# Hybrid encoder trunk on one core: gate tiles kept in DRAM until paced steps take them, and queries, keys and probabilities turned by DRAM and 32x32 block transposes in place of tensor-engine transposes

## The chip, the core and the metric

The kernel runs on one core of a Trainium2 chip. The core has a tensor engine (PE, with its weight loads shown as PEld), a vector engine (DVE), a scalar engine (ACT), GpSimd (POOL), a sync engine (SP, which issues the weight loads) and 16 DMA engines. Each engine takes its instructions in one fixed order. The metric is the device time of one execution in microseconds, the median of several runs. Before the change it is 1943.53 us (three runs, 1942.93 to 1944.33).

## What is computed

Two layers, each over 256 tokens of width 2048 in float32. One input projection feeds a convolution branch and an attention branch; both are gated, projected, merged and projected again.

```python
def conv_branch(a, glu, gate, conv_w, conv_b, ln_g, ln_b):
    u = a * jax.nn.sigmoid(glu)
    u = lax.conv_general_dilated(u, conv_w[:, None, :], ...) + conv_b   # depthwise, causal, width 31
    u = jax.nn.silu(layernorm(u, ln_g, ln_b))
    return u * jax.nn.silu(gate)

def mla_branch(...):
    q = (rmsnorm(q_down, q_a_g) @ w_uq).reshape(B, S, 16, 192)
    kv = (rmsnorm(kv_down, kv_a_g) @ w_ukv).reshape(B, S, 16, 128 + 128)
    ...                       # shared rotary key, per-head norm of q and k, rotary on the last 64
    o = chunk_causal_attention(q, k, v)
    return o.reshape(B, S, 2048) * jax.nn.silu(gate)

def hybrid_layer(x, ...):
    proj = rmsnorm(x, norm_g) @ w_in
    ...
    y = jax.nn.sigmoid(g_conv) * y_conv + jax.nn.sigmoid(g_mla) * y_mla
    return x + y @ w_out
```

## The kernel before

Tokens are two tiles of 128 (`t`), the model's width 16 tiles of 128. Every large product is taken in float32r from split operands: a value is a high part `hi` (a float32r cast) and a low part `lo` (value minus `hi`), and a product is three matmuls, hi by hi, hi by lo and lo by hi (lines 217 to 219). `product` (line 205) does one block of up to 512 columns. It goes through K in steps of two tiles; a step is called a slot here: 12 matmuls, then `background()`. Before each slot `split` makes the weights' halves from the loaded tile `raw`: ACT casts `hi` (line 178), DVE subtracts `lo` (line 179). `hi` and `lo` have three buffers each, and splits are issued two slots ahead, with a raised priority. In a layer the splits are numbered in order, 344 to a layer: 24 for the down block, then 8 for GLU block 0, and for each pair of heads `b` 2 for `uq`, 2 for `ukv` and 8 for the next GLU block; then 8 for each of the 28 blocks of the gates and output products. In the text, lo118 is the low half for split 118.

A framework records the instructions, orders them on each engine by priority and by times of its own, and fixes that order when the kernel is built. It also places the semaphores. `tc.issue_after(ins)` keeps instructions behind `ins` on its engine.

Work beside the products comes in two queues. `background()` (line 191) runs one step of `attn` at every slot, and as much of `fill` as a budget allows: `budget["rate"]` is added per slot, and every step has a cost. `fill` holds the convolution's taps (`tap`, line 634; two DVE operations of 128x256 each, line 646) and the layer norm (`mean`, `centre`, `var`, `apply`). What is left of `fill` is drained before the first `cgate` block.

There are two ways to turn a tile from tokens-on-partitions to channels-on-partitions. `turn` (line 230) writes the tile to DRAM by four DMAs on GpSimd (line 237), fetches it by a fifth (line 242), and at a later split, put in `deferred`, a DVE transpose of 32x32 blocks (line 246) ends it. GLU products and most gate blocks use it. The other way is PE: a matmul with the identity into PSUM, then a split copy out of PSUM.

Attention of a pair is eight steps at eight slots: `stats` (norm factors, scaled keys, rotary parts), `turn_rope` and `turn_nope` for queries and for keys (PE transposes at lines 526 and 513, then the splits), `scores`, `turn_p` (PE transposes of the probabilities, lines 588 to 592, then splits) and `values`. The last block of each set of gates (`turn4`, `c == 3`) also goes by PE (line 714).

The evacuations `uq_evac` and `ukv_evac` copy queries, keys and values of a pair out of the accumulators, of which there are four; the tiles `q`, `k` and `r` have two buffers.

Of the kernel before, what the change touches and what calls it, by code (L numbers as in the profile page):

```python
# [59 lines left out]
TURNED_AFTER = 6  # L60
SUMS_AFTER = 1
# [34 lines left out]
def trunk(ctx: ExitStack, tc: tile.TileContext, xT, x, g_in, pos, win, wuq, wukv, wpc, wpm, wo, cst, rows, invf, out):  # L96
# [13 lines left out]
    turn_d = pool("turn", 4, space=bass.MemoryType.DRAM)  # L110
    acc_p = pool("acc", 4, space=PSUM)
# [27 lines left out]
    for l in range(DEPTH):  # L139
# [12 lines left out]
    loaded, done = {}, {}  # L152
# [16 lines left out]
    def split(i):  # L169
# [10 lines left out]
        done[i] = hi, lo  # L180
        while deferred and deferred[0][0] <= i:
            with tc.issue_after(ins.ins):
                deferred.popleft()[1]()
# [5 lines left out]
    budget = {"fill": 0.0, "rate": 0.0}  # L189
# [40 lines left out]
    def turn(src, n, use, dst=None):  # L230

        e = n // 4
        d = turn_d.tile([4, 32, 4, e], F32, tag=f"t{n}", name="turn_d")
        for i in range(4):
# [3 lines left out]
            )  # L240
        z = wide_p.tile([P, 4, n // P, 32], F32, tag="w", name="turned")
        nc.gpsimd.dma_start(z.rearrange("p i c s -> p (i c s)"), d.rearrange("j s i e -> (j s) (i e)"))
# [119 lines left out]
    for l in range(DEPTH):  # L362
# [85 lines left out]
        def pair_of(b, pairs=pairs, v_split=v_split):  # L448
            if b not in pairs:
                pairs[b] = dict(  # L450
                    q=work2.tile([P, T, 2, QK], F32, tag="q", name="q"),
                    k=work2.tile([P, T, 2, NOPE], F32, tag="k", name="k"),
                    r=work2.tile([P, 2, T, 2, ROPE], F32, tag="r", name="r"),
# [6 lines left out]
        def uq_evac(b, t, ps, pair_of=pair_of):  # L460
            p = pair_of(b)
            nc.scalar.copy(p["q"][:, t].rearrange("p h d -> p (h d)"), ps)
            for h in range(2):
                junk = work.tile([P, 512], F32, tag="junk", name="junk")
                nc.scalar.activation(
                    junk[:, :QK], ps[:, h * QK : (h + 1) * QK], AF.Square, accum_out=p["ss"][:, 0, t, h : h + 1]
                )

        def ukv_evac(b, t, ps, pair_of=pair_of):
            p = pair_of(b)  # L470
            v = ps.rearrange("p (h a d) -> p h a d", h=2, a=2)
            nc.scalar.copy(p["vh"][:, t], v[:, :, 1, :])
            nc.vector.tensor_sub(p["vl"][:, t], v[:, :, 1, :], p["vh"][:, t].bitcast(F32))
            nc.scalar.copy(p["k"][:, t], v[:, :, 0, :])
            for h in range(2):
                junk = work.tile([P, 512], F32, tag="junk", name="junk")
                nc.scalar.activation(junk[:, :NOPE], v[:, h, 0, :], AF.Square, accum_out=p["ss"][:, 1, t, h : h + 1])

        def attention(b, pair_of=pair_of, ss_d=ss_d, kpe=kpe, ccq=ccq, ssq_t=ssq_t, gqk=gqk, nope_t=nope_t, rope_t=rope_t, rope_k=rope_k, rope_l=rope_l, o_sb=o_sb, pt_h=pt_h, pt_l=pt_l, rinv=rinv):
# [3 lines left out]
            def stats():  # L483
                ss, q, k = p["ss"], p["q"], p["k"]
# [7 lines left out]
                rk = r[:, 1].unsqueeze(3)  # L492
                nc.vector.tensor_mul(k, k, rk.broadcast_to([P, T, 2, NOPE]))
                nc.vector.tensor_mul(
                    p["r"][:, 1], kpe.unsqueeze(2).broadcast_to([P, T, 2, ROPE]), rk.broadcast_to([P, T, 2, ROPE])
                )
                qr = q[:, :, :, NOPE:]
                qa = work.tile([P, T, 2, ROPE], F32, tag="qa", name="qa")
                qb = work.tile([P, T, 2, ROPE], F32, tag="qb", name="qb")
                nc.vector.tensor_mul(qa, qr, ccq.unsqueeze(2).broadcast_to([P, T, 2, ROPE]))  # L500
                nc.vector.tensor_mul(qb, qr, ssq_t.unsqueeze(2).broadcast_to([P, T, 2, ROPE]))
                qr = p["r"][:, 0]
                nc.vector.tensor_sub(qr[:, :, :, :HALF], qa[:, :, :, :HALF], qb[:, :, :, HALF:])
                nc.vector.tensor_add(qr[:, :, :, HALF:], qb[:, :, :, :HALF], qa[:, :, :, HALF:])
# [3 lines left out]
            def turn_nope(which):  # L508
                src = p["qk"[which]]
                tp = tp_p.tile([P, 2, SEQ], F32, tag="tp", name="tp_qk")  # L510
                for h in range(2):
                    for t in range(T):
                        nc.tensor.transpose(tp[:, h, t * P : (t + 1) * P], src[:, t, h, :NOPE], ident)  # L513
                hi, lo = nope_t[:, 2 * which], nope_t[:, 2 * which + 1]
                if which == 0:
                    nc.scalar.activation(hi, tp, AF.Copy, scale=gqk)
                    nc.vector.scalar_tensor_tensor(lo, tp, gqk, hi.bitcast(F32), op0=ALU.mult, op1=ALU.subtract)
                else:
                    nc.scalar.copy(hi, tp)
                    nc.vector.tensor_sub(lo, tp, hi.bitcast(F32))  # L520

            def turn_rope(which):
                src = p["r"][:, which]
# [298 lines left out]
        for kind, i, pl in planned:  # L822
# [28 lines left out]
            elif kind == "mgate":  # L851
                budget["rate"] = 0.85
                if i == 3:
                    drain(attn)
# [103 lines left out]
```

## Time and profile before

| | |
|---|---|
| median of three runs | 1943.53 us (1942.93 to 1944.33) |
| the profiled execution | 1944.69 us, of which the span is 1942.9 |
| PE busy | 1927.0 us, 99% |
| DVE busy | 1583.7 us, 82% |
| ACT busy | 1096.6 us, 56% |
| GpSimd busy | 222.7 us, 11% |
| mean granted PE clock | 0.996 |

How to read the lines. A line of a timeline is start and duration in us, engine, source line, operation, the tile written and those read, shapes and count; in brackets stands the engine's idle time just before it and what ended it. A line of a group is the operation with its count, then busy time in us and mean ns of one, then idle time before it. A line of waits is who waited for whom: us in total, times, longest. A line of windows is the stretch, its length, then busy us and count for PE, PEld, DVE, ACT and POOL, then the granted clock, the share of the DMA engines and GB/s. Matmuls are pipelined, so their durations overlap, and their starts tell more.

### The profile page before, as it was taken

Reading aid. Unit: us, or ns where it says so; the run is one execution under the profiler, and the core shown is the slowest. Engines: PE = TensorE matmul, PEld = TensorE weight load, DVE = VectorE, ACT = ScalarE, POOL = GpSimd, SP = SyncE. Lnnn points to the kernel's source line nnn. Section 1 sums busy time; section 2 is a strip of 40 time slices with the busy share of each in tenths; the row PEclk is TensorE's granted clock in tenths of the full one; section 3 lists DMA queues with packets and bytes.
Section 4 is the critical chain, followed back from the end, with each engine's and each line's share of the span. In section 5 each row is a group of like instructions: output and inputs, shape, how many; then the busy total and the mean of one; then the engine's idle time right before and its main releaser. Section 6 shows DMA issues by size and latency. Waiting matters only on the chain.

```text
span 1942.9 us, 25501 instructions
## 1 busy us (share of the span) xinstructions
PE 1927.0 (99%) x9085; PEld 1627.9 (84%) x9085; DVE 1583.7 (82%) x2816; ACT 1096.6 (56%) x1745; POOL 222.7 (11%) x424
## 2 busy tenths in 40 slices
PE   9999999999999999999999999999999999999999
PEld 8888888888888887888898888888888888878887
DVE  7789988999998787666657899889999987876654
ACT  6667767665444446444556676776554434454443
POOL 0111111121000001121301121121200000022200
PEclk9999999999999999999999999999999999999999
DMA  8655545566555555666865455555665555566674
GB/s 292 217 178 182 195 167 180 197 217 222 195 195 195 195 195 186 231 243 229 277 230 197 176 195 177 179 182 195 225 210 195 194 195 195 181 210 231 241 255 141
DMA packets 71760, 397.72 MB, mean 205 GB/s; under 512 B 12736, under 2 KB 12752, under 8 KB 32720
## 3 DMA queue, kind: packets, MB, share of 16 engines
q1 hardware_dynamic: 55728, 361.44, 52.7%
q0 software_dynamic: 15904, 34.65, 5.6%
q8 instruction: 71, 1.16, 0.2%
q14 instruction: 57, 0.47, 0.1%
HBM read 375.59 MB, written 20.45 MB: 204 GB/s over the span
## 4 chain that ended last, share of the span: by engine, by line
PE 97%; DVE 1%; DMA 1%; issue 0%; ACT 0%; SPq 0%; POOL 0%; DVEq 0%
PE acc L218 31%; PE acc L219 31%; PE acc L217 31%; PE o_ps L604 1%; PE s L558 1%; PE tp_qk L513 1%; DMA turned<-turn_d 0%; DVE lo L179 0%; DVE v_t L672 0%; PE tp_rope L526 0%; DMA raw<-in_win 0%; PE s L544 0%; PE tp L714 0%; PE s L542 0%; PE tp_p L588 0%
## 5 line engine op out<-in xcount | busy, mean ns | idle before, releaser
L178 ACT CAST hi<-raw 128x1024 fp32r<-128x1024 f32 (+2 forms) x688 | 704.6, 1025 | 726.8 <-PE acc L219 507.2
L179 DVE TENSOR_TENSOR lo<-raw,hi 128x1024 fp32r<-128x1024 f32 (+2 forms) x688 | 815.6, 1188 | 268.7 <-ACT hi L178 265.9
L646 DVE SCALAR_TENSOR_TENSOR v_t<-u_t,cst,v_t 128x256 f32<-128x256 f32 x960 | 413.9, 478 | 1.1
L218 PE MATMUL acc<-lo,h_hi 128*128 128x512 f32 (+2 forms) x864 | 334.8, 388 | 1.4 <-DVE lo L179 1.4
L218 PE MATMUL acc<-lo,hT 128*128 128x512 f32 (+2 forms) x864 | 333.7, 386 | 2.4 <-DVE lo L179 2.4
L219 PE MATMUL acc<-hi,h_lo 128*128 128x512 f32 (+2 forms) x864 | 332.4, 385 | 0.0
L219 PE MATMUL acc<-hi,hT 128*128 128x512 f32 (+2 forms) x864 | 331.6, 384 | 0.0
L217 PE MATMUL acc<-hi,h_hi 128*128 128x512 f32 (+2 forms) x864 | 303.7, 386 | 4.8 <-ACT hi L178 4.8
L217 PE MATMUL acc<-hi,hT 128*128 128x512 f32 (+2 forms) x864 | 303.1, 384 | 1.6 <-ACT hi L178 1.6
L217 PEld LDWEIGHTS acc<-hi,h_hi 128*128 128x128 f32 x864 | 162.3, 189 | 35.1 <-ACT hi L178 5.6
L218 PEld LDWEIGHTS acc<-lo,hT 128*128 128x128 f32 x864 | 162.7, 188 | 32.5 <-DVE lo L179 3.6
L218 PEld LDWEIGHTS acc<-lo,h_hi 128*128 128x128 f32 x864 | 163.3, 189 | 31.8 <-DVE lo L179 2.7
L217 PEld LDWEIGHTS acc<-hi,hT 128*128 128x128 f32 x864 | 161.6, 188 | 31.6 <-ACT hi L178 2.1
L219 PEld LDWEIGHTS acc<-hi,h_lo 128*128 128x128 f32 x864 | 163.5, 189 | 29.2
L219 PEld LDWEIGHTS acc<-hi,hT 128*128 128x128 f32 x864 | 162.8, 188 | 29.1
L237 POOL DMA_DIRECT2D turn_d<-gate x160 | 87.0, 550 | 571.4 <-ACT gate L769 345.0
L237 POOL DMA_DIRECT2D turn_d<-su x128 | 69.6, 550 | 477.9 <-DVE su L626 467.7
L218 PE MATMUL acc<-lo,yT 128*128 128x512 f32 x256 | 100.0, 390 | 0.0
L218 PE MATMUL acc<-lo,ycT 128*128 128x512 f32 x256 | 99.6, 390 | 0.0
L219 PE MATMUL acc<-hi,yT 128*128 128x512 f32 x256 | 99.6, 389 | 0.0
L218 PE MATMUL acc<-lo,oT 128*128 128x512 f32 x256 | 99.6, 389 | 0.0
L219 PE MATMUL acc<-hi,oT 128*128 128x512 f32 x256 | 99.6, 389 | 0.0
(204 smaller groups left out, 2487.6 us busy)
## 6 DMA issues: line engine op xcount, KB each, us to landing
raw<-in_win SPq DMA_DIRECT2D x192, 1024.0 KB, 4.8
raw<-in_wpm SPq DMA_DIRECT2D x32, 1024.0 KB, 4.7
raw<-in_wpc SPq DMA_DIRECT2D x32, 1024.0 KB, 4.8
raw<-in_wo SPq DMA_DIRECT2D x32, 1024.0 KB, 5.1
raw<-in_wukv SPq DMA_DIRECT2D x16, 1024.0 KB, 4.7
raw<-in_wuq SPq DMA_DIRECT2D x16, 768.0 KB, 4.2
turned<-turn_d POOLq DMA_DIRECT2D x46, 256.0 KB, 4.4
raw<-in_win SPq DMA_DIRECT2D x15, 768.0 KB, 6.4
```

The lines of the kernel that those rows point to most:

```text
L178: nc.scalar.copy(hi, r)
L179: ins = nc.vector.tensor_sub(lo, r, hi.bitcast(F32))
L217: nc.tensor.matmul(pts[t][:, :n], sh, hi[:, kk, :], start=first, stop=False)
L218: nc.tensor.matmul(pts[t][:, :n], sh, lo[:, kk, :], start=False, stop=False)
L219: nc.tensor.matmul(pts[t][:, :n], sl, hi[:, kk, :], start=False, stop=last)
L237: nc.gpsimd.dma_start(d[:, :, i, :].rearrange("j s e -> s j e"), src[32 * i : 32 * i + 32, :].rearrange("s (j e) -> s j e", j=4),)
L513: nc.tensor.transpose(tp[:, h, t * P : (t + 1) * P], src[:, t, h, :NOPE], ident)
L558: nc.tensor.matmul(s1[:, h, :], qa, ka, start=n == 0, stop=n == len(terms) - 1)
L604: nc.tensor.matmul(o_ps[:, h, kt * P :], v[j][:, kt, h, :], pt[i][:, h, queries], start=n == 0, stop=n == len(todo) - 1,)
L646: nc.vector.scalar_tensor_tensor(dst, src, w, dst, op0=ALU.mult, op1=ALU.add)
```

## The change

- Queries and keys are no longer turned on PE. The columns of `w_uq` and `w_ukv` are reordered on the host so that a pair's values stand in one tile `qk` of six 32-wide groups by four. `stats` ends by parking both token tiles (768 wide) in DRAM and fetching them back turned by blocks; `blockwise` then transposes 32x32 blocks on DVE in place, and `split_rope` and `split_nope` make hi and lo from SBUF. `scores` writes the probabilities in the same arrangement, parks and fetches them, and `split_p` transposes and splits.
- Attention's steps get slots: `at_slot(ahead, f)` runs `f` in the background call so many slots on. Between `stats` and `blockwise` are six slots, and six between `scores` and `split_p`. Steps that are left are run before the last `mgate` block.
- The four blocks of the convolution gate go ahead of those of the merge gate (`cgate` ahead of `gconv`). Its turned tiles are parked in DRAM (pool `park`, eight buffers), also for the last block; the multiplications by the gate (`gated`) become steps of `fill`, fetched two blocks ahead.
- The fill rate in the GLU stage is 0.55 in place of 0.65; from the first `mgate` block on it is what is left divided by the slots left of 156, and the drain moves from the first `cgate` to the first `pconv` block.

```diff
         for kind, s in (
             ("mgate", "win"), ("gmla", "win"), ("pmla", "wpm"),
-            ("gconv", "win"), ("cgate", "win"), ("pconv", "wpc"), ("wout", "wo"),
+            ("cgate", "win"), ("gconv", "win"), ("pconv", "wpc"), ("wout", "wo"),
...
+    def at_slot(ahead, f):
+        steps.append((clock[0] + ahead, f))
+
     def background():
+        clock[0] += 1
         if attn:
             attn.popleft()()
+        due = [f for slot, f in steps if slot <= clock[0]]
+        steps[:] = [e for e in steps if e[0] > clock[0]]
+        for f in due:
+            f()
+        if budget["slots"]:
+            budget["rate"] = max(sum(cost for cost, _ in fill), 0.0) / budget["slots"]
+            budget["slots"] -= 1
...
+    def park(src, n, home):
+        d = home.tile([4, 32, 4, n // 4], F32, tag=f"t{n}", name="turn_d")
         for i in range(4):
             nc.gpsimd.dma_start(
                 d[:, :, i, :].rearrange("j s e -> s j e"),
                 src[32 * i : 32 * i + 32, :].rearrange("s (j e) -> s j e", j=4),
             )
+        return d
+
+    def fetch(d, z):
+        nc.gpsimd.dma_start(z, d.rearrange("j s i e -> (j s) (i e)"))
...
+                qk=work2.tile([P, T, 4, 6, 32], F32, tag="qk", name="qk"),
+                qr=work2.tile([P, T, 2, 2, HALF], F32, tag="qr", name="qr"),
...
+                for t in range(T):
+                    rows = qk[:, t].rearrange("p j i c -> p (j i c)")
+                    fetch(park(rows, 768, turn_d), rows)
...
-            def turn_nope(which):
-                src = p["qk"[which]]
-                tp = tp_p.tile([P, 2, SEQ], F32, tag="tp", name="tp_qk")
-                for h in range(2):
-                    for t in range(T):
-                        nc.tensor.transpose(tp[:, h, t * P : (t + 1) * P], src[:, t, h, :NOPE], ident)
...
+            def blockwise():
+                for t in range(T):
+                    z = p["qk"][:, t].rearrange("p j i c -> p (j i c)")
+                    with tc.issue_after(newest[0]):
+                        nc.vector.transpose(z, z)
+
+            def split_nope(which):
+                z = back[:, :, 2 * which : 2 * which + 2, :].rearrange("p b h s -> p h b s")
+                hi, lo = (nope_t[:, 2 * which + i].rearrange("p h (b s) -> p h b s", s=32) for i in range(2))
                 if which == 0:
...
+                    nc.scalar.activation(z, z, AF.Copy, scale=gqk)
+                nc.scalar.copy(hi, z)
+                nc.vector.tensor_sub(lo, z, hi.bitcast(F32))
...
-            def turn_p():
...
+                st["pr"] = pr.rearrange("p j h x c -> p (j h x c)")
+                fetch(park(st["pr"], 768, turn_d), st["pr"])
+
+            def split_p():
+                z = st["pr"]
+                with tc.issue_after(newest[0]):
+                    nc.vector.transpose(z, z)
+                z = z.rearrange("p (b i s) -> p i b s", i=6, s=32)
+                hi, lo = (a.rearrange("p h (x b s) -> p (h x) b s", x=3, s=32) for a in (pt_h, pt_l))
+                nc.scalar.copy(hi, z)
+                nc.vector.tensor_sub(lo, z, hi.bitcast(F32))
...
+            at_slot(0, stats)
+            at_slot(QK_AFTER, lambda: (blockwise(), split_rope(0), split_rope(1)))
+            for which in range(2):
+                at_slot(QK_AFTER + 1 + which, lambda which=which: split_nope(which))
+            at_slot(QK_AFTER + 3, scores)
+            at_slot(QK_AFTER + 3 + P_AFTER, split_p)
+            at_slot(QK_AFTER + 4 + P_AFTER, values)
...
+            def ahead(c):
+                gates[c] = [fetched(d, 512) for d in keep["parked"][c]]
+
             fill.append((4.5, var))
+            for c in range(2):
+                fill.append((0.1, lambda c=c: ahead(c)))
             for b in range(8):
                 fill.append((0.7, lambda b=b: apply(b)))
+            for c in range(4):
+                for t in range(T):
+                    fill.append((1.5, lambda c=c, t=t: gated(c, t, gates[c][t])))
+                if c < 2:
+                    fill.append((0.1, lambda c=c: ahead(c + 2)))
...
             elif kind == "glu":
-                budget["rate"] = 0.65
+                budget["rate"] = 0.55
...
             elif kind == "mgate":
-                budget["rate"] = 0.85
+                if i == 0:
+                    budget["slots"] = 20 * 8 - 4
...
             elif kind == "cgate":
-                if i == 0:
-                    drain(fill)
...
             elif kind == "pconv":
                 if i == 0:
                     drain(fill)
+                    budget["slots"] = 0
```

More of the change, by code (lines that the diff above doesn't have):

```diff
@@ L60 @@
 TURNED_AFTER = 6
+QK_AFTER = 6
+P_AFTER = 6
 SUMS_AFTER = 1
@@ L110, in trunk @@
     turn_d = pool("turn", 4, space=bass.MemoryType.DRAM)
+    park_d = pool("park", 8, space=bass.MemoryType.DRAM)
     acc_p = pool("acc", 4, space=PSUM)
@@ L522, in turn_rope @@
[L522 to L526 removed]
+                for t in range(T):
+                    rk = r[:, 1, t, :]
+                    k = qk[:, t, :, 2:4, :]
+                    nc.vector.tensor_mul(k, k, rk.unsqueeze(1).unsqueeze(3).broadcast_to([P, 4, 2, 32]))
+                    nc.vector.tensor_mul(
+                        qk[:, t, :, 5, :].rearrange("p (h a) c -> p h a c", h=2),
+                        kpe[:, t].rearrange("p (a c) -> p a c", a=2).unsqueeze(1).broadcast_to([P, 2, 2, HALF]),
+                        rk.unsqueeze(2).unsqueeze(3).broadcast_to([P, 2, 2, HALF]),
+                    )
```

178 lines of the change are left out of this document (85 added, 93 removed).

## The prediction

> **What bounds the kernel now.** I read the page's totals and chain first, then what the tensor engine waits for, then the stages one by one, then single instructions.
>
> ```profile
> span 1942.9 us, 25501 instructions
> PE 1927.0 (99%) x9085; PEld 1627.9 (84%) x9085; DVE 1583.7 (82%) x2816; ACT 1096.6 (56%) x1745; POOL 222.7 (11%) x424
> ...
> DMA packets 71760, 397.72 MB, mean 205 GB/s; under 512 B 12736, under 2 KB 12752, under 8 KB 32720
> ...
> PE 97%; DVE 1%; DMA 1%; issue 0%; ACT 0%; SPq 0%; POOL 0%; DVEq 0%
> ```
>
> The tensor engine (PE) is the chain: 97% of it. Its waits are few:
>
> ```profile
> PE acc L217 <- ACT hi L178: 6.4, 3, 3.1
> PE acc L218 <- DVE lo L179: 3.7, 5, 1.4
> ```
>
> That is 10.1 us; the longest, 3.1, falls in the start. By stage (us, then busy time per engine):
>
> ```profile
> 84.00:424.00 340.00, 340.00 (x1711) 290.44 (x1710) 302.21 (x635) 239.74 (x492) 55.31 (x107) 1.00 0.55 187
> 720.00:765.00 45.00, 41.98 (x173) 33.63 (x172) 38.29 (x56) 28.43 (x42) 5.45 (x10) 0.94 0.54 186
> ```
>
> 84 to 424 is the stage of attention and GLU in layer 0: PE never idles, and DVE (third pair) is busy 302 of 340. 720 to 765 is the only place inside layer 0 where PE waits, and the granted clock falls to 0.94 there: the remaining fill is drained in one go.
>
> **What the removed work is worth.** A transpose's duration is not its price, since matmuls overlap. The starts tell it:
>
> ```profile
> 196.75 0.39 PE L217 MATMUL acc<-hi,qkc 128*128 128x512 f32 x1
> 196.98 0.60 PE L513 MATMUL tp_qk<-ident,k 128*128 128x128 f32 x4
> 197.34 0.47 PE L218 MATMUL acc<-lo,qkc 128*128 128x512 f32 x1
> 197.65 0.39 PE L219 MATMUL acc<-hi,qkc 128*128 128x512 f32 x1
> ```
>
> A product of 512 columns starts 0.23 us after the one before. From 196.98 to 197.65 are 0.67 us with one product in it, so four transposes cost 0.44, or 0.11 each. Each pair of heads has 4+4 for the no-position parts, 2+2 for the rotary parts and 6 for the probabilities: 18 x 16 pairs = 288; the gate's last block had 2 x 4 in each layer: 16. 304 x 0.11 = **-33.4 us**, all of it on PE. In the built order 304 tensor instructions are indeed gone, so a change that does nothing is excluded.
>
> The drained fill is the second term:
>
> ```profile
> 756.28 0.39 PE L219 MATMUL acc<-hi,h_lo 128*128 128x512 f32 x1
> 758.32 0.74 PE L217 MATMUL acc<-hi,h_hi 128*128 128x512 f32 x2 [1.64 <-ACT hi L178]
> 760.22 0.79 PE L218 MATMUL acc<-lo,h_hi 128*128 128x512 f32 x1 [1.17 <-DVE lo L179]
> 760.81 0.63 PE L219 MATMUL acc<-hi,h_lo 128*128 128x512 f32 x1
> 761.24 0.63 PE L217 MATMUL acc<-hi,h_hi 128*128 128x512 f32 x1
> ...
> 765.93 0.55 PE L219 MATMUL acc<-hi,h_lo 128*128 128x512 f32 x1
> ```
>
> Two waits of 2.8 us together, and then products 0.43 apart in place of 0.23 until 765.9: 13 x 0.2 = 2.6 us of slower clock. So 5.4 in layer 0; the same place in layer 1 I put at the same, 11 for both. The fill is now paced over 156 slots, so I take **-11 us** off, and add back below what the new order makes of that place (between 0 and -11 if it all returns).
>
> On the clock: the row slows after waits of 1.6 and 1.2 us. The Trainium skill, "TensorE: Matmul & The Clock Gate", section "What's actually happening", says that the array falls to half rate after about 3.4 us of idle and needs as much work to return. The trace agrees on half rate, not on so long an idle. By the page alone only the six longest waits below would slow the clock, and the sum would come to 1975 (a rival below).
>
> **What the change adds, as work.** Per pair DVE gets three block transposes of 768. Rows for its prices:
>
> ```profile
> L246 DVE STREAM_TRANSPOSE turned<-turned 128x512 f32<-128x512 f32 x46 | 32.2, 704 | 8.3 <-DMA turned<-turn_d 5.6 <-issue 2.1 <-DMA turn_d<-gate 0.5
> L473 DVE TENSOR_TENSOR pv<-acc,pv 128x256 fp32r<-128x256 f32 x32 | 13.4, 418 | 0.6 <-ACT pv L472 0.4
> L263 DVE SCALAR_TENSOR_TENSOR r_p<-rsq_t,r_p 128x8 f32<-128x8 f32 x48 | 7.6, 159 | 1.0
> 218.72 2.06 DVE L646 SCALAR_TENSOR_TENSOR v_t<-u_t,cst,v_t 128x256 f32<-128x256 f32 x5
> 220.71 0.95 DVE L179 TENSOR_TENSOR lo<-raw,hi 128x768 fp32r<-128x768 f32 x1
> ...
> 725.34 4.91 DVE L672 TENSOR_TENSOR v_t<-v_t,ln_stats 128x512 f32<-128x512 f32 x8
> 730.17 1.22 DVE L179 TENSOR_TENSOR lo<-raw,hi 128x1024 fp32r<-128x1024 f32 x1
> 731.30 0.69 DVE L678 TENSOR_TENSOR s<-s,sq 128x512 f32<-128x512 f32 x1
> ```
>
> Starts again: a tap is 0.40 (5 in 1.99), an operation of 512 is 0.60 (8 in 4.83), a split's lo is 1.13. Durations overlap by 0.08, so 256 wide is 0.34, and 768 wide, at the same slope, 0.88. Three transposes are 2.6 us a pair, 42 us in all, beside 2.5 for the gate's last block. That would fit: I added up these prices over DVE's built order, between the split that opens the first GLU block and the one that opens the first gate block (96 splits). Before it is 248 us of DVE work against 281 of PE work; after, 249 against 268, since the GLU rate falls from 0.65 to 0.55 and moves taps out. DVE stays below PE on average. Cost of the work as such: 0, with PE's products as its cover.
>
> DMA too is covered: each pair adds three turns of 0.39 MB out and back, 38 MB in all, beside the 397.7 MB of the run, with the DMA engines at 0.55 in that stage. GpSimd gains 240 issues of 0.55 us, 132 us on an engine busy 223 of 1943. The swap of the two gates and the tiles kept in DRAM issue as many writes and fetches as before but for the last block's 20; cover as above, cost 0. The DVE and ACT work of splitting and normalising is only reshaped.
>
> **What it adds, as order.** Here is the loss. PE needs a new hi and lo every slot of twelve products, and there are three buffers of each, so DVE can run ahead only so far:
>
> ```profile
> 739.28 0.62 PE L217 MATMUL acc<-hi,h_hi 128*128 128x512 f32 x2
> 742.00 0.62 PE L217 MATMUL acc<-hi,h_hi 128*128 128x512 f32 x2
> ...
> 742.21 1.05 ACT L178 CAST hi<-raw 128x1024 fp32r<-128x1024 f32 x1 [1.66 <-PE acc L219]
> ...
> 743.29 1.23 DVE L179 TENSOR_TENSOR lo<-raw,hi 128x1024 fp32r<-128x1024 f32 x1 [1.49 <-ACT hi L178]
> ```
>
> A slot is 2.72 us. ACT starts hi when a buffer comes free (742.21), lo ends at 744.5, 2.3 later; that buffer is needed two slots after it came free, 5.44. The greatest lead is 3.2 us. Whatever stands between one lo and the next beyond slot plus lead stops PE.
>
> In the order before, no gap in the attention stage holds more than 5.5 us of DVE work, and PE never waited there. In the changed order a pair's turned tiles arrive together, and everything that waited for them stands in one block: between lo118 and lo119 stand the transposes of both query/key tiles and the low part of the probabilities (3 x 0.88), ten taps (4.0), two value splits and a GLU product (3 x 0.34), four rotary splits (4 x 0.34), two splits of 512 (2 x 0.60): 10.2, and 11.3 with lo119. PE has six products (1.36 us) before it needs lo119: 11.3 - 1.4 - 3.2 = **6.8 us** of waiting. The same sum gives, in layer 0, 1.7, 3.5, 5.1, 6.8 and 0.7 (lo80, 95, 107, 119, 131) and in layer 1 0.8, 4.7, 0.7, 6.0, 7.1, 1.8 and 0.7; with 0.6 each at the gate multiplies it is 41. That is the lower bound: lateness also carries from one split to the next. A running sum over all splits gives 84, with the lead at 3.2, and 64 if the lead is taken 1 us longer, as the small operations (0.19 when dependent, 0.16 long in the row above) overlap partly. The old order by the same two sums has 10.3 and 4.1 where 7.0 us were measured after the start. I take **+64**: 50 in the attention stages, 13 where applying the norm and gating now crowd into one GCONV block.
>
> The clock makes each longer wait dearer. Six or seven waits a layer are over 2 us; at 2.0 each (the 2.6 above, less what a slower PE gives DVE to catch up): **+25 us**, with 0 and 35 as ends.
>
> Then the trip itself. The block transpose waits for its fetch, and all lo's queue behind it on DVE.
>
> ```profile
> 225.73 2.17 POOL L237 DMA_DIRECT2D turn_d<-su  x4 [20.78 <-DVE su L626]
> 229.75 0.56 POOL L242 DMA_DIRECT2D turned<-turn_d  x1 [1.85 <-DMA turn_d<-su]
> turned<-turn_d POOLq DMA_DIRECT2D x46, 256.0 KB, 4.4
> turn_d<-gate POOLq DMA_DIRECT2D x160, 64.0 KB, 3.0
> ```
>
> Four issues take 2.2 us, landing 3.0, a fetch 0.55 and 4.4 for two thirds of the new size. On GpSimd the probabilities' four writes of one pair stand ahead of the eight writes of the next pair's queries and keys: 2.2 + 4.4 + 3.0 + 1.1 + some 5 = 15.7 us from the exponentials to the landing. The order leaves six or seven slots between, 16 us or more. I take 0, with 4 us a pair for the 12 pairs in the middle (+48) as the upper end.
>
> **The sum**, against the profiled execution's own 1944.7 us (its span and 1.8 around it): 1944.7 - 33.4 - 11 + 64 + 25 = 1989. That execution is 1.2 above the median of the runs, so I predict **1988 us**.
>
> **Rivals.**
> - *The bursts are hidden* (13%). If PE never waits for lo: 1944.7 - 33.4 = 1911, or 1900 without the drain. For it: DVE's average stays below PE's. Against it: 10 us of DVE work in one gap, which three buffers cannot cover.
> - *The bursts cost about what the transposes cost* (11%): the single gaps alone, 41, no carry, clock at 0: 1944.7 - 33.4 - 11 + 41 = 1941, to 1955 with part of the clock.
> - *Only long waits slow the clock* (14%): the row that slowed may owe it to two waits close together. With 2.0 for the six single gaps over 3.4 us alone, 12 in place of 25: 1975. The Trainium skill's rule on the clock, above, is this one.
> - *The round trip decides* (12%): GpSimd's queue is a loop, scores to probabilities to the next pair's queries. A period of PE work is about 35 us now; when exponentials, 15.7 of trip, transposes, splits and scores together pass it, every pair is late: 1988 + 48 = 2036.
>
> **How the numbers follow.** My forecast, bursts that stop PE and slow its clock, 1955 to 2025, has 50%; with the rival on the clock, which lies inside it, 64%. The range 1935 to 2045 leaves out the first rival and a little at the top. Within 0.2% (some 4 us, about what a measurement here tells from no change) comes only from the middle rival: 4%. Faster, 14%: the first rival and a sliver of the second. Slower, 82%.
>
> **What would show it.** Right: waits of products on lo or hi of 3 to 8 us, once per pair from the third pair on, in both attention stages, with products 0.43 apart behind them; no transposes of q, k, p on PE; DVE's transposes of 768 near 0.95 long. Wrong: PE at full pace through 84 to 420 (then the lead is longer than 3.2), or DVE idle at its block transposes until the fetch (then the trip decides), or waits at the products that lie with the accumulators, not with the splits.

## The result and the profile after

The changed kernel takes 2011.87 us (median of four runs, 2009.33 to 2013.53), the kernel before 1943.93 (four runs, 1942.93 to 1944.44): a ratio of 1.0347, 95% interval 1.0334 to 1.036. It is 68 us slower; 1988 was forecast, in a range of 1935 to 2045, so the forecast was 24 us short. The profiled execution took 2011.23 us, its span 2009.5.

The page of the changed kernel, totals, clock and DMA:

```profile
span 2009.5 us, 25453 instructions
PE 1931.5 (96%) x8781; PEld 1618.9 (81%) x8781; DVE 1622.8 (81%) x2884; ACT 1116.8 (56%) x1782; POOL 364.0 (18%) x684
PEclk9999989999999999999999999888999999999999
DMA packets 85650, 437.58 MB, mean 218 GB/s; under 512 B 16896, under 2 KB 19984, under 8 KB 46608
```

PE has the 304 matmuls fewer that the forecast counted, yet it is busy 4.5 us longer than before, and the clock row has dips that it had not. With 0.11 us a transpose taken off, PE's own pace has cost 1931.5 - (1927.0 - 33.4) = 37.9 us. The rest is waiting. What PE waited for (us in total, times, longest), all rows of 3 us and more:

```profile
PE acc L235 <- DVE lo L182: 13.0, 17, 1.3
PE acc L234 <- DVE su L666: 9.9, 8, 3.0
PE s L602 <- ACT qk_t L565: 9.9, 4, 3.4
PE o_ps L642 <- DVE pv L633: 9.0, 7, 2.7
PE acc L234 <- ACT hi L181: 8.4, 8, 2.8
PE acc L234 <- ACT gate L788: 8.0, 4, 3.0
PE s L602 <- ACT qk_t L577: 5.7, 4, 2.4
PE o_ps L642 <- ACT pv L632: 3.9, 2, 2.6
```

All rows together are 73.1 us, where the kernel before had 11.7. Only 21.4 of it is for `hi` and `lo`; the larger part is for accumulators that `su` or `gate` still had to empty, for the halves of queries and keys (`qk_t`) and of the probabilities (`pv`). The span grew by 66.6: -33.4 for the transposes, +37.9 for the pace, +61.4 for waits, +0.7 of idle time in no row.

Where it happens, by windows (stretch, length, then busy us and count of PE, PEld, DVE, ACT, POOL, clock, DMA share, GB/s):

```profile
84.00:460.00 376.00, 343.65 (x1571) 287.07 (x1570) 308.21 (x632) 242.53 (x496) 117.50 (x222) 0.96 0.64 218
460.00:790.00 330.00, 330.00 (x1469) 273.57 (x1468) 313.31 (x529) 162.61 (x181) 33.42 (x63) 1.00 0.61 211
790.00:860.00 70.00, 67.50 (x293) 54.29 (x292) 46.79 (x61) 41.50 (x54) 3.82 (x7) 1.00 0.56 200
1105.00:1475.00 370.00, 337.90 (x1526) 283.17 (x1525) 304.10 (x612) 234.42 (x469) 112.97 (x210) 0.94 0.63 216
```

The two attention stages (first and last row) hold 32 us of waits each and the low clock. From 460 to 790, where the drained fill used to stop PE, it never idles now. One of the stops, on VectorE's timeline of the changed kernel:

```profile
305.85 0.97 DVE L629 STREAM_TRANSPOSE pr<-pr 128x768 f32<-128x768 f32 x1
306.75 0.93 DVE L558 STREAM_TRANSPOSE qk<-qk 128x768 f32<-128x768 f32 x1
307.61 1.18 DVE L182 TENSOR_TENSOR lo<-raw,hi 128x1024 fp32r<-128x1024 f32 x1
308.71 0.95 DVE L633 TENSOR_TENSOR pv<-pr,pv 128x768 fp32r<-128x768 f32 x1
...
310.37 0.97 DVE L558 STREAM_TRANSPOSE qk<-qk 128x768 f32<-128x768 f32 x1
...
312.80 0.87 DVE L575 TENSOR_TENSOR qk_t<-qk,qk_t 64x256 fp32r<-64x256 f32 x2
...
316.23 0.48 DVE L666 SCALAR_TENSOR_TENSOR su<-acc,rinv_x,su 128x256 f32<-128x256 f32 x1
...
320.90 1.22 DVE L182 TENSOR_TENSOR lo<-raw,hi 128x1024 fp32r<-128x1024 f32 x1
```

From one `lo` at 307.61 to the next at 320.90 VectorE works 13.3 us with hardly a gap: the probabilities of one pair, the queries and keys of the next, and the GLU tile that would free an accumulator, one behind the other. PE at the same place:

```profile
309.71 1.41 PE L642 MATMUL o_ps<-pv 128*128 128x128 f32 x10 [1.19 <-DVE pv L633]
313.53 0.38 PE L602 MATMUL s<-qk_t 128*128 128x256 f32 x1 [2.40 <-ACT qk_t L577]
314.17 0.46 PE L586 MATMUL s<-qk_t 128*128 128x256 f32 x1 [0.26 <-DVE qk_t L578]
316.85 0.66 PE L234 MATMUL acc<-hi,qkc 128*128 128x384 f32 x1 [2.22 <-DVE su L666]
317.31 0.52 PE L235 MATMUL acc<-lo,qkc 128*128 128x384 f32 x1
317.63 0.52 PE L236 MATMUL acc<-hi,qkc 128*128 128x384 f32 x1
```

Four waits, 6.1 us, and behind them products of 384 columns 0.32 us apart, where at 308.0 they started 0.17 apart. Why both trips come back at once stands on GpSimd's timeline:

```profile
288.57 2.18 POOL L250 DMA_DIRECT2D turn_d<-pr  x4 [8.79 <-ACT pr L616]
290.74 4.34 POOL L250 DMA_DIRECT2D turn_d<-qk  x8
296.58 0.56 POOL L257 DMA_DIRECT2D pr<-turn_d  x1 [1.50 <-DMA turn_d<-qk]
297.65 0.55 POOL L257 DMA_DIRECT2D qk<-turn_d  x1 [0.51 <-DMA turn_d<-qk]
```

GpSimd stands 8.79 us until ScalarE has the exponentials. The next pair's queries and keys stand behind these writes; on VectorE's timeline the last operation on such a tile before them (L545) ends at 281.8. They are sent at 290.74, nine microseconds later (6.8 until the probabilities' writes start, and 2.2 for these four issues), right behind the probabilities, and the two are read back one microsecond apart. Over the whole run:

```profile
POOL turn_d L250 <- ACT pr L616: 183.0, 16, 19.4
...
ACT pv L505 <- PE o_ps L642: 25.6, 11, 4.8
...
DVE qk L558 <- DMA qk<-turn_d: 5.2, 3, 2.4
DVE pr L629 <- DMA pr<-turn_d: 2.7, 2, 1.5
```

GpSimd waits 183 us at the probabilities' writes. ScalarE waits 25.6 us, 11 times and in 9 of the 16 pairs, to write a pair's values (line 505) until PE has read the values of the pair two before (`o_ps`): there are two buffers of them. VectorE itself waits some 8 us for what comes back. The trip is seldom late at the instruction that takes it. Whether the damage is in what was put together around it is for the experiments.

### The profile page after: what moved, and what is told of

It reads as the page before. It is cut to its first block, busy times and chain, and to the rows that moved or that the text cites. A ratio compares the mean times of both kernels' runs of the same rounds, so it can differ in the third digit from the quotient of the medians.

```text
span 2009.5 us, 25453 instructions
## 1 busy us (share of the span) xinstructions
PE 1931.5 (96%) x8781; PEld 1618.9 (81%) x8781; DVE 1622.8 (81%) x2884; ACT 1116.8 (56%) x1782; POOL 364.0 (18%) x684
## 2 busy tenths in 40 slices
DMA packets 85650, 437.58 MB, mean 218 GB/s; under 512 B 16896, under 2 KB 19984, under 8 KB 46608
## 5 line engine op out<-in xcount | busy, mean ns | idle before, releaser
L181 ACT CAST hi<-raw 128x1024 fp32r<-128x1024 f32 (+2 forms) x688 | 702.8, 1024 | 763.7 <-PE acc L236 558.3
L250 POOL DMA_DIRECT2D turn_d<-gate x176 | 95.8, 551 | 699.9 <-ACT gate L821 467.5
L234 PE MATMUL acc<-hi,qkc 128*128 128x384 f32 (+1 forms) x256 | 97.0, 394 | 11.8 <-DVE su L666 9.9
L235 PE MATMUL acc<-lo,qkc 128*128 128x384 f32 (+1 forms) x256 | 98.9, 386 | 1.1 <-DVE lo L182 1.0
```

The costliest lines, as they stand in the source:

```text
L181: nc.scalar.copy(hi, r)
L234: nc.tensor.matmul(pts[t][:, :n], sh, hi[:, kk, :], start=first, stop=False)
L235: nc.tensor.matmul(pts[t][:, :n], sh, lo[:, kk, :], start=False, stop=False)
L250: nc.gpsimd.dma_start(d[:, :, i, :].rearrange("j s e -> s j e"), src[32 * i : 32 * i + 32, :].rearrange("s (j e) -> s j e", j=4),)
```

## The experiments

Each time is a median beside runs of the kernel before on the same chip, with its ratio. A column gives the forecast's sum over the built order, for the attention stages and with the lead at 4.2 us, beside PE's measured waits in these stages (84 to 460 and 1080 to 1475). The built sum is worked out from the order and the prices, not measured. Pace is PE's busy time over 1927.0 once 0.11 us is allowed for each matmul that is gone. Waits and pace are those of the profiled execution, which can lie some microseconds from the median (e11's, at 1948.12, was the shortest of its six).

| kernel | us | ratio (95%) | built sum | waits there | all waits | pace |
|---|---|---|---|---|---|---|
| before | 1943.93 | 1 | 0.0 | 0 | 11.7 | 0 |
| changed | 2011.87 | 1.0347 (1.0334-1.036) | 48.7 | 63.9 | 73.1 | 37.9 |
| e1 gate part alone | 1943.32 | 0.9988 (0.9976-1.0) | 0.0 | 0 | 10.0 | -0.8 |
| e2 probabilities on PE | 1958.82 | 1.0073 (1.0057-1.009) | 15.1 | 22.5 | 39.4 | 13.4 |
| e3 queries, keys on PE | 1978.70 | 1.0173 (1.0158-1.0189) | 9.8 | 18.3 | 39.8 | 13.1 |
| e4 no trip | 1934.55 | 0.995 (0.9935-0.9965) | 28.2 | 15.6 | 29.0 | 5.9 |
| e5 third v buffer | 2004.00 | 1.0302 (1.0287-1.0317) | 43.6 | 43.2 | 64.4 | 37.0 |
| e6 idle trip | 1977.77 | 1.0176 (1.0157-1.0196) | 31.5 | 24.8 | 53.6 | 20.1 |
| e7 P written by ScalarE | 1987.39 | 1.0226 (1.0208-1.0244) | 29.8 | 44.6 | 57.0 | 29.0 |
| e8 = e5 and e7 | 1963.81 | 1.0097 (1.008-1.0114) | 19.3 | 30.1 | 40.8 | 23.5 |
| e9 = e8, q and k written by SyncE | 1986.83 | 1.0217 (1.0203-1.0231) | 11.9 | 43.0 | 60.2 | 26.5 |
| e10 = e3 with e8's edits | 1960.85 | 1.0087 (1.0073-1.01) | 0.6 | 12.0 | 30.4 | 8.9 |
| e11 = e7, read back aside | 1951.99 | 1.0039 (1.0026-1.0052) | 24.2 | 23.6 | 34.4 | 14.0 |
| e12 = e8, eight slots for P | 1960.31 | 1.0092 (1.0066-1.0118) | 14.4 | 37.2 | 49.6 | 21.2 |

**The parts of the change, e1 to e4.** e1 has the gate's parking, its order and the paced fill, and leaves attention as before. e2 and e3 are the changed kernel with one of the two turns back on PE; the cut is e2's, and e3 does the same for queries and keys:

```diff
-                fetch(park(st["pr"], 768, turn_d), st["pr"])
...
+            def turn_p():
...
+                    nc.tensor.transpose(tp0[:, h, :P], pr[h], ident)
```

> The kernel before with the convolution gate's part of the change alone (gate tiles in DRAM, paced fill, cgate ahead of gconv); queries, keys and probabilities stay on PE, and the GLU rate stays 0.65. Theory: the drained fill's waits and slow clock (11 us) go, and 16 transposes of 0.11 (1.8 us): 1931. Rival: the paced steps crowd again at the end of gconv and stop PE there: 1944 or more, with waits of 2 to 7 us there.

> The changed kernel with the probabilities turned on PE again (96 transposes back, 10.6 us of PE). Theory of the block (what stops PE is the work that stands together when the turned tiles arrive): the block between two lo's is smaller, attention waits fall from 64 to some 25 us and the clock's loss to 15: 1950. Theory of the trip (GpSimd's loop from probabilities to the next pair's queries): the loop is cut and the waits go altogether: 1915.

> The changed kernel with queries and keys turned on PE again (192 transposes back, 21 us of PE); the probabilities still go by DRAM. Theory of the block: waits of 10 to 16 us and 8 of clock remain: 1945. Theory of the trip: one trip of about 11 us a pair is still in the chain and still late: 1965 or more.

The gate part is worth next to nothing, 0.9988: 12 us above the 1931 of its theory, at the rival's time but without the rival's waits of 2 to 7 us (the longest at the gates is 1.2). e2, at 1958.8, lies above both its theories and nearer the block's, e3, at 1978.7, where the trip's put it. With e1 as the base (its GLU rate is still 0.65), the probabilities' way costs 1978.7 - 1943.3 = 35 us, that of queries and keys 1958.8 - 1943.3 = 16, and both 69: 18 us more than the sum. Something between the two must make them dearer together. e4 keeps every transpose and split on VectorE and ScalarE and drops the trip, so rows go into the transposes unsent:

```diff
-                    fetch(park(rows, 768, turn_d), rows)
+                    pass
...
-                fetch(park(st["pr"], 768, turn_d), st["pr"])
```

> The changed kernel without the passage through DRAM of queries, keys and probabilities: their tiles are transposed by blocks where they stand, so the blocks themselves are not exchanged (the attention computes with scrambled operands). PE's work and DVE's are those of the changed kernel. Theory of the block: the work still comes in blocks, waits of 28 to 40 us and some 20 of clock stay: 1955 to 1965. Theory of the trip: the waits of attention go: 1905.

1934.55: neither theory gave this. The trip is worth 2011.87 - 1934.55 = 77 us, though VectorE waits for it some 8 us, and what VectorE gained in work is cheap. The first attention stage of e4, by windows:

```profile
84.00:460.00 376.00, 368.04 (x1751) 310.13 (x1750) 351.93 (x717) 266.56 (x531) 64.91 (x125) 1.00 0.58 194
```

VectorE is busy 351.93 of 376 us, more than the 308.21 of the changed kernel, and PE loses 8 us, not 32. VectorE's throughput isn't the bound. The long blocks are gone too: in the attention stages no two `lo` start more than 6.9 us apart in e4, nor more than 6.4 before the change, while the changed kernel has nine stretches over 9 us, the longest 16.3. VectorE's instructions don't get slower by the transfers either: a `lo` of 1024 takes 1219 ns with the trip, 1217 without, a transpose of 768 968 and 964.

**Buffers or traffic, e5 and e6.** e5 gives the values a third buffer, in columns that two tiles leave over:

```diff
+        v_split.append([a[:, 3584:].rearrange("p (t h d) -> p t h d", t=T, h=2) for a in (pv, qk_t)])
-                    vh=v_split[b % 2][0],
+                    vh=v_split[b % 3][0],
```

> The changed kernel with a third buffer for the split values (v hi and lo), in columns that two tiles leave unused; nothing else differs. Ring theory: the values of a pair can be written only when the products with the probabilities of the pair two before have been read, so the two trips through DRAM close a loop of two pair periods (24 splits, some 65 us); the ScalarE row that waits for the product o_ps at the writing of pv (25.6 us in 11 waits) goes below 5 us, TensorE's waits fall from 73 us towards the 29 us of the kernel without the trip, the clock is over 0.99, and the time is 1935 to 1955. Block theory of the prediction: the built order still has 53 us of lateness from long stretches of VectorE work between one lo and the next, against 65, so the time falls by some 15 us only, to about 1997. Theory that the transfers themselves disturb: 2012, no change.

The ring alone fails: 2004.0, between the 1997 of the block and the 2012 of the transfers, and the row that it was to remove shrank from 25.6 to 13.9 us, while others grew. ScalarE's waits in e5:

```profile
ACT pv L633 <- DVE pr L630: 20.0, 7, 7.0
ACT pv L506 <- PE o_ps L643: 13.9, 4, 4.0
ACT qk L491 <- DVE qk_t L567: 10.5, 8, 2.8
```

The probabilities still come late, and now the two `qk` buffers are short too. e6 is e4 with DMAs of the same bytes that nobody waits for:

```diff
+        def idle_trip():
+            with tc.issue_after(newest[0]):
+                d = park(x768, 768, turn_d).rearrange("j s i e -> (j s) (i e)")
+                nc.gpsimd.dma_start(spare[0], d[:, :512])
+                nc.gpsimd.dma_start(spare[1][:, :256], d[:, 512:])
```

> The kernel without the trip (1934.6), and beside it the same DMAs as the trip has, of the same bytes and from the same queue at the same slots, but of data that nobody waits for: 128x768 of the layer's input to DRAM in four writes and back in two reads, into columns that are never read; queries, keys and probabilities stay unturned, so the attention's output is not the reference's. Ring and block theories, in which the trip costs by its length and order: 1933 to 1945. Theory that the trip costs by its traffic (DMA engines, GpSimd's issuing, SBUF ports): most of the 77 us comes back, 1975 to 2010.

1977.77, which speaks for traffic until one looks where it was lost. Of the 24.6 us of waits that e6 has more than e4 (53.6 against 29.0), 9.2 lie in the attention stages (24.8 against 15.6). The start and the layer boundary, by windows of e6:

```profile
0.00:84.00 84.00, 77.07 (x387) 70.19 (x388) 57.74 (x151) 50.00 (x92) 49.11 (x95) 0.98 0.95 351
...
860.00:1105.00 245.00, 230.56 (x1085) 198.68 (x1084) 145.76 (x227) 119.25 (x192) 101.78 (x189) 0.97 0.79 268
```

GpSimd (fifth pair) is busy 49 us in the first stretch and 102 at the boundary, against 3.5 and 38.6 in e4: with nothing to wait for, the DMAs were issued in heaps ahead of their stage, where they stood in the way of the layer's own transfers. The run doesn't settle the question; e11 asks it again with the writes at their places.

**The queue, e7 and e8.** One argument moves the probabilities' four writes to the engine that computes them:

```diff
-    def park(src, n, home):
+    def park(src, n, home, q=nc.gpsimd):
...
-                fetch(park(st["pr"], 768, turn_d), st["pr"])
+                fetch(park(st["pr"], 768, turn_d, nc.scalar), st["pr"])
```

> The changed kernel with one edit: the four writes that park a pair's probabilities are issued on ScalarE's queue, right behind the exponentials that ScalarE itself computes, not on GpSimd's; the read back stays on GpSimd's queue; bytes and transfers are the same. Theory of the queue: GpSimd issues in order, and stands 183 us in 16 waits (19.4 us the longest) at these writes until the exponentials are done, with the next pair's queries and keys and the convolution's turns behind it; that makes the trips long and the work of two pairs fall together. With lo and hi due in stretches of VectorE's built order at a lead of 4.2 us, the attention stages come to 30 us of waits against 49 (the runs so far measured 64 for 49, 43 for 44, 23 for 15): waits in the attention stages near 35 us, time 1965 to 1985. Theory that the transfers themselves disturb (DMA traffic or ports): no change, 2005 to 2015.

> Both the third buffer for the split values and the probabilities' writes on ScalarE's queue. Theory of the queue and the built order: stretches at a lead of 4.2 us come to 19 us in the attention stages, so waits there near 25 us and a time of 1950 to 1968. If the two edits act apart, their gains add: -8 of the third buffer on top of what the queue alone gives. Theory that the transfers disturb: 2004 as with the third buffer alone.

The bytes are the same, 437.58 MB. The queue alone gives 24 us, and with the third buffer 48, where the two by themselves give 24 + 8. That fits a loop in which, with one way open, the other still held. The long blocks go with it: of the nine stretches over 9 us between two `lo`, e5 still has nine, e7 six and e8 three.

The one argument changes more than the place in the queue. GpSimd also issues less (330.5 us busy in place of 364.0), and ScalarE's writes go by another kind of DMA queue (91794 packets in the run in place of 85650), though they land no sooner: 3.3 us after their issue, 2.5 before. No run separates these; the nine microseconds of delay shown above, 6.8 of waiting and 2.2 of issuing, put the place in the queue first. e7 ends just above its range. GpSimd now stands 71.0 us at the writes of queries and keys until VectorE has made them, and here:

```profile
POOL pr L257 <- DMA turn_d<-pr: 101.2, 11, 19.5
```

GpSimd's timeline in e8, one pair:

```profile
269.79 4.36 POOL L250 DMA_DIRECT2D turn_d<-qk  x8
285.25 0.57 POOL L257 DMA_DIRECT2D pr<-turn_d  x1 [11.10 <-ACT hi L181]
285.82 0.56 POOL L257 DMA_DIRECT2D qk<-turn_d  x1
```

Queries and keys are sent at 269.79, 1.6 us after VectorE's last operation on such a tile (ends at 268.2), not nine. But their read back still stands behind that of the probabilities, for 11 us.

**What is left, e9 to e12.** e9 also takes the writes of queries and keys off GpSimd; e10 tries for a kernel better than both, with only the probabilities by DRAM. The cut is e9's:

```diff
-                    fetch(park(rows, 768, turn_d), rows)
+                    fetch(park(rows, 768, turn_d, nc.sync), rows)
```

> The kernel with three buffers for the split values and the probabilities' writes on ScalarE's queue, and now also the queries' and keys' writes on SyncE's queue, so that GpSimd issues none of the trip's writes; the reads back stay with it. Theory of the queue: GpSimd's waits at the rows pr and qk go, VectorE's built stretches at a lead of 4.2 us come to 12 us in the attention stages against 19, and the time falls further, to 1938 to 1952; the kernel without the trip (1934.6) is its floor. Rival: SyncE issues in order too, and where it waits for the normalised queries and keys the weight loads behind it come late; then TensorE waits at hi and lo in the attention stages and the time is 1965 or more.

> Queries and keys turned on TensorE as before the change, the convolution gate parked as in the change, and only the probabilities by DRAM, with three buffers for the split values and the writes on ScalarE's queue. Built stretches at a lead of 4.2 us: 0.6 us in the attention stages (the kernel before: 0.0), with 96 transposes fewer than before at 0.11 us, 10.6 us. Theory of the queue and the buffers: the probabilities' trip then costs nothing, and the time is 1932 to 1942, below the kernel before. Theory that a trip through DRAM costs by itself: as with the probabilities alone by DRAM so far, 1975 to 1982.

e9 went the rival's way: 1986.83. PE's waits and SyncE's in e9:

```profile
PE acc L235 <- DVE lo L182: 26.6, 26, 3.4
PE acc L234 <- ACT hi L181: 11.3, 6, 4.5
...
SPq L250 <- DMA turn_d<-pr: 41.5, 11, 5.6
```

SyncE stands 41.5 us at the writes with the weight loads behind it (and the 128 issues take it 0.43 us each, the median), and waits for `hi` and `lo` go from 23.7 us in e8 to 37.9. Its built sum, 11.9, is the lowest of the versions that turn everything by DRAM, and the measured waits are 43.0: the sum knows nothing of loads that come late or of waits at the queue. e10 is a miss as well, 1960.85 where 1932 to 1942 was expected, and 1975 to 1982 by the other theory. VectorE's and GpSimd's waits in e10:

```profile
DVE pr L612 <- DMA pr<-turn_d: 9.2, 8, 1.5
...
POOL pr L257 <- ACT hi L181: 75.4, 5, 23.9
POOL pr L257 <- DMA turn_d<-pr: 70.1, 5, 23.8
```

Here VectorE does stand at the block transposes, in 8 pairs of 16, with every later `lo` behind it. A built order without a long block is not enough, then; e4, with a built sum of 28.2, shows that it isn't needed either. No version in this series beats the kernel before but e4, which leaves the trip out; e1 is level with it within 0.2%.

e11 is e7 with the reads landing where nobody looks, and e12 gives the probabilities two slots more in e8. The first two lines are e11's (the same is done for the probabilities), the last two e12's:

```diff
-                    fetch(park(rows, 768, turn_d), rows)
+                    fetch_aside(park(rows, 768, turn_d))
...
-P_AFTER = 6
+P_AFTER = 8
```

> The kernel with the probabilities' writes on ScalarE's queue (1987.4), with one edit: what is read back of queries, keys and probabilities lands in columns that nothing reads (512 of 768 columns), and VectorE's block transposes take the rows that were never sent, so nobody waits for the trip, while its writes stay as they are in bytes and place; the attention's output is not the reference's. Theory that the transfers disturb: it stays at 1980 to 1990. Theory that the trip costs by what waits for it and by the order that this gives: it falls to 1935 to 1948, next to the kernel without any trip (1934.6); built stretches at a lead of 4.2 us are 24 us in the attention stages, the kernel without the trip has 28.

> The kernel with three buffers for the split values and the probabilities' writes on ScalarE's queue (1963.8), with eight slots instead of six between the scores and the probabilities' split. If the probabilities still come late for their slot (GpSimd stands 48.7 us at their reads, 7 times), two slots more, some 5 us, take waits away: built stretches at a lead of 4.2 us are 14 us in the attention stages against 19, so 1952 to 1962. If slots are not what is short: 1962 to 1970.

e11's page and its first attention stage:

```profile
PE 1907.6 (98%) x8781; PEld 1597.2 (82%) x8781; DVE 1616.3 (83%) x2884; ACT 1115.4 (57%) x1782; POOL 330.2 (17%) x620
...
84.00:460.00 376.00, 364.72 (x1720) 304.98 (x1719) 344.77 (x702) 263.70 (x527) 109.99 (x207) 1.00 0.71 232
```

Writes at their places, GpSimd as busy as in e7, no stretch over 7.2 us between two `lo` in these stages, and 1951.99: 35 us below e7, 17 above e4. That is 4 us above the range of the theory of waiting and order, and far below that of the transfers. So, taken in this order, of the trip's 77 us, 24 come from the place of the probabilities' writes in GpSimd's queue (to e7), 35 from what waits for the reads and the order this gives (e7 to e11), and 17 from what e11 still has: the transfers, their issuing, and VectorE's wait until a tile has been sent before it is transposed in place (`DMA turn_d<-qk`, 7.1 us, 8 times). As e5, e7 and e8 do not add up, another order of the steps could share the 77 out otherwise, and each edit also gives a newly built order. The 17 would be more with whole tiles, as e11 reads back two thirds. e12, at 1960.31, lies in the range named for slots that are short, but within e8's uncertainty (1.0066 to 1.0118 against 1.008 to 1.0114), so the run doesn't decide it; if slots are short, they cost a few microseconds. Its profiled execution, at 1970.58, was the longest of its four, so its waits in the table are high.

## Why the prediction came out as it did

The number came out within the range, 24 us from the forecast, and blocks of VectorE's work stopped PE as forecast. But the step that put the trip at 0 beside them was wrong, and some terms came right only in their sum, which is luck.

**The transposes, -33.4.** Right. No run has the transposes alone, but stretches of 144 products of the same kinds in which PE never waits can be compared by their starts. The one with the first pair takes 32.27 us before the change (81.41 to 113.67) and 31.43 after it (82.39 to 113.81), with 8 transposes fewer. One with a whole pair's 18 transposes takes 36.88 us before (258.95 to 295.83) and in e4, without them, 34.99 (224.04 to 259.03). Both give 0.105 a transpose, 32 us for 304.

**The drain, -11, and +13 for the crowded gate block.** From 460 to 790 the waits are gone, and the crowd at the gate block, which was to cost 13 us, shows as 2.5 us of idle PE between 790 and 860 (2.4 in layer 1). But in e1, where this part stands by itself, the median gains 1.3 us and the profiled span 4.2, 1.8 of it from 16 transposes: the stop was made smaller there (3.0 to 2.1 us of waits in layer 0) and another came at 860 to 1080 (1.5). Both terms were too large, and that they cancelled was luck.

**VectorE's work, 0.** Right. e4 does all of it at 351.93 us of 376 and is below the kernel before.

**The blocks, +64.** The amount is right: with the drain's 5.6 of waits off, 58 us more waits were forecast, and 61.4 came. In part this is luck: the attention stages have 63.9 where 50 were forecast, the gate blocks 4.9 where 13 were. The lead by the forecast's own rows is 3.1 us (5.44 - 2.31), not 3.2, which changes a block by 0.1. The forecast's own example, lo118 to lo119, is the block after the one shown above, which is lo106 to lo107:

```profile
351.31 1.18 DVE L182 TENSOR_TENSOR lo<-raw,hi 128x1024 fp32r<-128x1024 f32 x1
363.22 1.23 DVE L182 TENSOR_TENSOR lo<-raw,hi 128x1024 fp32r<-128x1024 f32 x1
354.28 1.41 PE L642 MATMUL o_ps<-pv 128*128 128x128 f32 x10 [1.19 <-DVE pv L633]
358.66 0.62 PE L234 MATMUL acc<-hi,qkc 128*128 128x384 f32 x1 [2.97 <-DVE su L666]
```

It takes 11.9 us from one start to the next where 11.3 were worked out, with just the operations that the forecast listed, and PE waits 4.7 us where 6.8 were worked out: the two waits above and one of 0.49. In the block shown first it waits 6.1 where 5.1 were. The transposes are 0.93 to 0.97 long. Two things about the blocks were wrong. The place: of 73.1 us, 21.4 are for `hi` and `lo`. Most is for accumulators and attention's halves, which the forecast itself listed as a sign against it: in PE's order these products stand ahead of those that need the late `lo`. The sum over `lo` measured the crowd, not the queue in which PE met it: at lo118 to lo119 no wait is for `lo`. And the cause: the block was put down to VectorE's new work, but e4, with the same work, has no stretch over 6.9 us between two `lo`, and 15.6 us of waits in these stages. The forecast read a built order that already had the trip in it.

**The trip, 0, with +48 as the upper end, and the rival that it decides.** This step failed. The forecast worked out 15.7 us for the trip against 16 in the slots, and looked for lateness at the instruction that takes the data, where indeed little is lost. It named the loop through GpSimd's queue, scores to probabilities to the next pair's queries, and priced it as 48 us on top of the blocks. The runs show that the loop is what makes most of the blocks: e7 and e8 take 24 and 48 us away with the same bytes and the same number of instructions on VectorE, and the waits in the attention stages go from 63.9 to 44.6 and 30.1. It is no addition to the +64 but the larger part of it, together with the two buffers of values, which the forecast didn't mention.

The Trainium skill, "DMA: Bandwidth & Descriptors", section "Rules for kernel authors", says that spreading DMAs over SyncE, ScalarE and GpSimd doesn't help bandwidth and saves only issuing time. For bandwidth the runs agree: e7 moves the same 437.58 MB, and the writes it moved land no sooner. By that rule what e7 can gain is the issuing, 2.2 us a pair on GpSimd. In the block shown the wait that stood ahead of the next pair's writes was 6.8 us, three times as long, so the larger part of the 24 us is put down here to the place behind an instruction that waits; no run parts it from the issuing.

**The clock, +25, between 0 and 35.** Mis-sized: 37.9 us, beyond its upper end. With the drain's 5.2 of slow clock off, 20 was forecast, and the 18 missing are most of the 22 between the sum, 1989, and the profiled execution's 2011. The price was put on six or seven waits a layer over 2 us; the runs show that shorter waits in a row pay as well. Over the twelve runs with more waits than before (e1 aside), the pace grew by 0.34 to 0.81 us for each further us of waiting. Not all of the pace is the granted clock, though. From 0.996 to 0.981 of the span is some 30 us (an estimate: what is missing to 1, times the span), and e11, with 0.996 as before, still has a pace of 14.0; what the rest is stays open. The Trainium skill, "TensorE: Matmul & The Clock Gate", section "What's actually happening", has the array throttled after an idle window of about 3.4 us. In the block shown no single wait is that long, PE works 0.84 us in the 5.7 from 311.1 to 316.85, and then runs at half rate. That fits a window that counts work more than one that needs unbroken idle, but no run separates these.

## What to carry to other kernels

Before a tile is sent through DRAM, look at what stands behind the sending instruction on its queue: a write that waits for its data holds every trip behind it, and trips that leave together come back together. Here it paid to issue a write from the engine that computes its data (e7, 24 us), and it cost to put one on a queue that feeds others, as SyncE's does (e9, 23 us). And cost a change of this kind against the order built without the transfers as well as with them. Built sums of 28.2 and 48.7 would have said that the blocks are not the work alone, which a look at who waits for the transfer doesn't show; they would not have given the price, as the waits measured were 15.6 and 63.9.

## What was not expected of the hardware

Waits cost more than their length: with 61.4 us of them came 37.9 us of slower products, some 30 by the granted clock. The 31.5 MB that e11 moves more than e4 (431.29 against 399.79) cost, with their issues, 17 us, with the DMA engines at 0.71 of their time in the first attention stage and VectorE's instructions no longer than before. Some 7 us are waits of VectorE for tiles being sent. Whether the rest is weight loads that land later (5.0 us after their issue against 4.8 in e4, the median of the largest group), the convolution's turns behind more issues on GpSimd, or the order that the build makes of it, stays open.
